# A Gelu gate streamed through one core: every transfer in one order on one queue

## The chip, the cores and the metric

The kernel runs on one core of a Trainium2 chip. The metric is the device time of one execution in microseconds (us), as the median of several runs. Of the core's engines the kernel uses ScalarE (ACT) for Gelu, VectorE (DVE) for the product, and two engines that issue transfers: SyncE (SP) and ScalarE. Each of these two has a queue of its own (q1 for SyncE and q10 for ScalarE in the profile); the packets of both are carried by the core's 16 DMA engines.

## What is computed

The input is x of shape (32, 512, 2048) in float32. The last axis is cut in two halves, and the output of shape (32, 512, 1024) is the Gelu of the first half times the second:

```
x1, x2 = x[..., :1024], x[..., 1024:]
out = 0.5 * x1 * (1 + erf(x1 / sqrt(2))) * x2
```

134.2 MB are read and 67.1 MB are written, each byte once.

## The kernel before, in words

The 16,384 rows of x are cut into 16 tiles of 1024 rows. Each of the 128 partitions takes R = 8 neighbouring rows of a tile (lines 26 to 29). So one tile puts 64 KB of input into each partition, contiguous in memory, and takes 32 KB of output from it. There are two input buffers, `x_bufs`, and two output buffers, `o_bufs` (lines 30 and 31); tile i uses number i % 2 of both.

A tile goes through four steps. `load` (line 48) brings it in from SyncE's queue. ScalarE computes Gelu of the first half of each row from the input buffer into the output buffer (line 87). VectorE multiplies the output buffer in place by the second half of each row (line 95). `store` (line 53) waits for the multiply and sends the output buffer out. Gelu and multiply work in steps of 5 and 3 rows (line 79), so that VectorE starts while ScalarE does the second step.

The order of the work is written by hand with semaphores, and every engine takes its instructions in program order:

- SyncE's queue has load 0 as two halves of four rows each and load 1 at once, and then load i + 2 as soon as both multiplies of tile i are done (line 114), which frees the input buffer. It also has the stores of the last two tiles (lines 104 and 110).
- ScalarE's queue has the stores of tiles 0 to 13 (lines 107 and 112). Since ScalarE waits for the multiply before it issues a store, its next Gelu comes after that.
- ScalarE begins tile i when `ready[i % 2]` has counted all transfers before it on that buffer pair: load i, which fills the input buffer, and store i - 2, which frees the output buffer (line 85).
- Tile 0 starts on the first half of its load. The first and the last tile work in steps of 2, 2 and 4 rows and are stored in two halves (lines 79 and 103 to 107).
- The first instruction on ScalarE's queue is a small transfer of 8 packets of 512 bytes from x into a tile that nobody reads (`opening`, line 63).

At the end SyncE waits for the stores counted by `tail_stored` (line 125).

Of the kernel before, what the change touches and what calls it, by code (L numbers as in the profile page):

```python
# [1 line left out]

# [4 lines left out]

GELU = mybir.ActivationFunctionType.Gelu


@with_exitstack
def kernel(
    ctx: ExitStack,
    tc: tile.TileContext,
    x: bass.AP,
    out: bass.AP,
):
    nc = tc.nc
    P = nc.NUM_PARTITIONS

    x_flat = x.flatten_outer_dims()
    out_flat = out.flatten_outer_dims()
    n_rows, dim = x_flat.shape
    half = dim // 2

    R = 8
    x_t = x_flat.rearrange("(n p r) d -> n p r d", p=P, r=R)
    o_t = out_flat.rearrange("(n p r) d -> n p r d", p=P, r=R)
    n_tiles = x_t.shape[0]
    x_bufs = [nc.alloc_sbuf_tensor(f"x{k}_tile", [P, R, dim], x.dtype) for k in range(2)]  # L30
    o_bufs = [nc.alloc_sbuf_tensor(f"o{k}_tile", [P, R, half], out.dtype) for k in range(2)]

    first = [nc.alloc_semaphore(f"first{j}") for j in range(2)]
    ready = [nc.alloc_semaphore(f"ready{k}") for k in range(2)]
    gelu_done = nc.alloc_semaphore("gelu_done")
    mul_done = nc.alloc_semaphore("mul_done")
    tail_stored = nc.alloc_semaphore("tail_stored")
    opened = nc.alloc_semaphore("opened")  # L40
    scrap = nc.alloc_sbuf_tensor("scrap_tile", [8, 128], x.dtype)
    n = {sem.name: 0 for sem in [*first, *ready, gelu_done, mul_done, tail_stored, opened]}

    def counted(ins, sem, by):
        ins.then_inc(sem, by)
        n[sem.name] += by

    def load(i, rows, sem):
        ins = nc.sync.dma_start(out=x_bufs[i % 2][:, rows, :], in_=x_t[i][:, rows, :])  # L49
        counted(ins, sem, 16)  # L50
        return ins

    def store(queue, i, rows, sem):
        queue.wait_ge(mul_done, n[mul_done.name])
        counted(
            queue.dma_start(out=o_t[i][:, rows, :], in_=o_bufs[i % 2][:, rows, :]), sem, 16
        )

    opening = nc.scalar.dma_start(out=scrap[:, :], in_=x_t[0][:8, 0, :128])
    counted(opening, opened, 16)
    for ins in (
        opening,
        load(0, slice(0, 4), first[0]),
        load(0, slice(4, 8), first[1]),
        load(1, slice(0, 8), ready[1]),
    ):  # L70
        tc.no_tile_sem_insts.add(ins.ins.name)
    tc.close()
    tc.compile()  # L73

    for i in range(n_tiles):
        k = i % 2
        last = i == n_tiles - 1
        pieces = i == 0 or last
        steps = ((0, 2), (2, 4), (4, 8)) if pieces else ((0, 5), (5, 8))
        for lo, hi in steps:  # L80
            rows = slice(lo, hi)
            if i == 0 and lo % 4 == 0:
                nc.scalar.wait_ge(first[lo // 4], 16)
            elif lo == 0:
                nc.scalar.wait_ge(ready[k], n[ready[k].name])
            counted(
                nc.scalar.activation(  # L87
                    out=o_bufs[k][:, rows, :], in_=x_bufs[k][:, rows, :half], func=GELU
                ),
                gelu_done,  # L90
                1,
            )
            nc.vector.wait_ge(gelu_done, n[gelu_done.name])
            counted(
                nc.vector.tensor_mul(  # L95
                    out=o_bufs[k][:, rows, :],
                    in0=o_bufs[k][:, rows, :],
                    in1=x_bufs[k][:, rows, half:],
                ),
                mul_done,  # L100
                1,
            )
            if pieces and hi % 4 == 0:
                if last:
                    store(nc.sync, i, slice(hi - 4, hi), tail_stored)
                else:
                    store(nc.scalar, i, slice(hi - 4, hi), ready[k])
        if not pieces:
            if i == n_tiles - 2:
                store(nc.sync, i, slice(0, R), tail_stored)  # L110
            else:
                store(nc.scalar, i, slice(0, R), ready[k])
        if i + 2 < n_tiles:
            nc.sync.wait_ge(mul_done, n[mul_done.name])
            load(i + 2, slice(0, R), ready[k])


    nc.scalar.wait_ge(opened, 16)
    nc.scalar.drain()  # L119
    for sem in (*first, *ready, opened):  # L120
        nc.scalar.sem_clear(sem)
    nc.vector.drain()
    nc.vector.sem_clear(gelu_done)
    nc.sync.sem_clear(mul_done)
    nc.sync.wait_ge(tail_stored, n[tail_stored.name]).then_inc(
        tail_stored, -n[tail_stored.name]
    )


# [1 line left out]
_INS = ['x']  # L131
_OUTS = [((32, 512, 1024), 'float32')]


# [23 lines left out]
```

## Time and profile before

| | before |
|---|---|
| median of 3 runs | 469.25 us (469.18 to 469.42) |
| span of the profiled execution | 467.8 us |
| own time of the profiled execution | not listed apart from the three runs |
| DVE busy | 140.5 us (30%), 34 multiplies |
| ACT busy | 115.5 us (25%), 34 Gelus and one table load |
| DMA traffic | 201.34 MB, mean 430 GB/s over the span |
| Gelu of 5 rows, of 3 rows | 4469 ns, 2747 ns |
| multiply of 5 rows, of 3 rows | 5493 ns, 3351 ns |
| time from issue to landing, median | 44.4 us for a load, 44.7 us for a store on ScalarE's queue |

The span is the time from the first to the last thing that the profile records of the execution; a run's time holds a little more around it. Busy shares are averages over the span. The share of a DMA queue is the time that its packets took, as a share of the span of all 16 DMA engines. The chain of waits is followed back from the last instruction, at each step to what released it. Idle time of ScalarE and VectorE costs nothing in itself as long as the transfers go on.

### The profile page before, as it was taken

What the parts mean: (1) busy time and instruction counts of PE and PEld (TensorE: products, weight loads), DVE (VectorE), ACT (ScalarE), POOL (GpSimd) and SP (SyncE); (2) the same over time, 40 slices, a digit from 0 to 9 for tenths busy, and PEclk for the clock granted to TensorE, in tenths of its full rate; (3) what the DMA queues carried; (4) which work ended last, traced back from release to release, by engine and by line L of the source; (5) the groups of instructions that cost most, each with busy time, mean ns of one, the idle gap of its engine ahead of it and who ended that gap; (6) DMA issues with size and microseconds to landing.
All of it is one profiled execution on the core that took longest, in us unless ns stands there. A gap on an engine that the chain in (4) does not pass through costs nothing.

```text
span 467.8 us, 154 instructions
## 1 busy us (share of the span) xinstructions
DVE 140.5 (30%) x34; ACT 115.5 (25%) x35; POOL 0.2 (0%) x4
## 2 busy tenths in 40 slices
DVE  0330515207051060511606115060150702507043
ACT  1320606041060410604105050050501506014060
POOL 0000000000000000000000000000000000000000
DMA  8999999999999999999999999999999999999988
GB/s 359 448 448 448 398 406 496 403 403 448 459 437 403 440 412 493 403 403 448 487 409 403 445 406 493 403 403 448 493 403 403 448 426 471 403 426 426 493 384 379
DMA packets 5057, 201.34 MB, mean 430 GB/s; under 512 B 568, under 2 KB 576, under 8 KB 576
## 3 DMA queue, kind: packets, MB, share of 16 engines
q1 hardware_dynamic: 2880, 142.61, 70.6%
q10 hardware_dynamic: 2176, 58.73, 29.1%
q14 instruction: 1, 0.01, 0.0%
HBM read 134.22 MB, written 67.11 MB: 430 GB/s over the span
## 4 chain that ended last, share of the span: by engine, by line
DMA 76%; DVE 14%; ACT 8%; ACTq 0%; SPq 0%; issue 0%
DMA out_dram<-o_tile 66%; DVE o_tile L95 14%; DMA x_tile<-in_x_dram 10%; ACT o_tile L87 8%; ACTq L119 0%; SPq L49 0%
## 5 line engine op out<-in xcount | busy, mean ns | idle before, releaser
L95 DVE TENSOR_TENSOR o_tile<-o_tile,x_tile 128x5120 f32<-128x5120 f32 (+3 forms) x34 | 140.5, 4171 | 319.7 <-ACT o_tile L87 319.7
L87 ACT ACTIVATE o_tile<-x_tile 128x5120 f32<-128x5120 f32 (+3 forms) x34 | 114.3, 3407 | 337.3 <-DMA out_dram<-o_tile 301.8
L87 ACT ACT_TABLE_LOAD x1 | 1.3, 1283 | 2.9 <-PEq L73 2.9
L142 POOL MEMSET const-bfloat16-1.0<- 128x1 bf16 x1 | 0.1, 102 | 0.0
L142 POOL MEMSET const-uint8-127<- 128x1 uint8 x1 | 0.1, 101 | 0.0
L142 POOL MEMSET const-float32-0.0<- 128x1 f32 x1 | 0.1, 99 | 0.2 <-issue 0.2
L142 POOL MEMSET const-float32-1.0<- 128x1 f32 x1 | 0.1, 98 | 0.0
## 6 DMA issues: line engine op xcount, KB each, us to landing
out_dram<-o_tile ACTq DMA_DIRECT2D x13, 4096.0 KB, 44.7
x_tile<-in_x_dram SPq DMA_DIRECT2D x2, 4096.0 KB, 16.7
out_dram<-o_tile ACTq DMA_DIRECT2D x2, 2048.0 KB, 34.4
out_dram<-o_tile SPq DMA_DIRECT2D x1, 4096.0 KB, 25.2
out_dram<-o_tile SPq DMA_DIRECT2D x2, 2048.0 KB, 7.8
x_tile<-in_x_dram SPq DMA_DIRECT2D x15, 44.4
scrap_tile<-in_x_dram ACTq DMA_DIRECT2D x1, 4.0 KB
```

The costliest lines, as they stand in the source:

```text
L87: nc.scalar.activation(out=o_bufs[k][:, rows, :], in_=x_bufs[k][:, rows, :half], func=GELU),
L95: nc.vector.tensor_mul(out=o_bufs[k][:, rows, :], in0=o_bufs[k][:, rows, :], in1=x_bufs[k][:, rows, half:],),
L142: nc = _bacc.Bacc("TRN2", target_bir_lowering=False, num_devices=1)
```

## The change

All transfers now go out on SyncE's queue, in one order: load 0, load 1, then store i and load i + 2 in turn, and at the end load 14, load 15, store 13, store 14 and store 15. Each tile has one load and one store: the halves of the first and the last tile are gone, and so are their steps of 2, 2 and 4 rows; every tile works in steps of 5 and 3 rows. The opening transfer and its tile are gone.

The output of the last tile, number 15, goes to the input buffer of tile 14 in place of its own output buffer, which tile 13's store still reads. It uses the first 32 KB of that buffer in each partition. ScalarE waits for tile 14's multiply before it begins there. Load 15 is issued ahead of store 13, and the last three stores are counted by `tail_stored`.

```diff
+    last = n_tiles - 1
+
+    def out_tile(i):
+        if i == last:
+            return x_bufs[(i - 1) % 2].rearrange("p r d -> p (r d)")[:, : R * half].rearrange(
+                "p (r d) -> p r d", r=R
+            )
+        return o_bufs[i % 2]
...
-    def store(queue, i, rows, sem):
-        queue.wait_ge(mul_done, n[mul_done.name])
-        counted(
-            queue.dma_start(out=o_t[i][:, rows, :], in_=o_bufs[i % 2][:, rows, :]), sem, 16
-        )
+    def store(i, rows, sem):
+        nc.sync.wait_ge(mul_done, n[mul_done.name])
+        counted(nc.sync.dma_start(out=o_t[i][:, rows, :], in_=out_tile(i)[:, rows, :]), sem, 16)
...
-    opening = nc.scalar.dma_start(out=scrap[:, :], in_=x_t[0][:8, 0, :128])
-    counted(opening, opened, 16)
-    for ins in (
-        opening,
-        load(0, slice(0, 4), first[0]),
-        load(0, slice(4, 8), first[1]),
-        load(1, slice(0, 8), ready[1]),
-    ):
+    for ins in (load(0, slice(0, R), ready[0]), load(1, slice(0, R), ready[1])):
...
-        last = i == n_tiles - 1
-        pieces = i == 0 or last
-        steps = ((0, 2), (2, 4), (4, 8)) if pieces else ((0, 5), (5, 8))
-        for lo, hi in steps:
+        nc.scalar.wait_ge(ready[k], n[ready[k].name])
+        if i == last:
+            nc.scalar.wait_ge(mul_done, n[mul_done.name])
+        for lo, hi in ((0, 5), (5, 8)):
...
-            if i == n_tiles - 2:
-                store(nc.sync, i, slice(0, R), tail_stored)
-            else:
-                store(nc.scalar, i, slice(0, R), ready[k])
-        if i + 2 < n_tiles:
+        if i == last - 2:
             nc.sync.wait_ge(mul_done, n[mul_done.name])
+            load(last, slice(0, R), ready[k])
+            store(i, slice(0, R), tail_stored)
+        elif i > last - 2:
+            store(i, slice(0, R), tail_stored)
+        else:
+            store(i, slice(0, R), ready[k])
             load(i + 2, slice(0, R), ready[k])
```

Gelu and multiply take their output from `out_tile(i)` in place of `o_bufs[k]`.

More of the change, by code (lines that the diff above doesn't have):

```diff
@@ L31 @@
     o_bufs = [nc.alloc_sbuf_tensor(f"o{k}_tile", [P, R, half], out.dtype) for k in range(2)]
-    first = [nc.alloc_semaphore(f"first{j}") for j in range(2)]
     ready = [nc.alloc_semaphore(f"ready{k}") for k in range(2)]
@@ L39 @@
     tail_stored = nc.alloc_semaphore("tail_stored")
-    opened = nc.alloc_semaphore("opened")
-    scrap = nc.alloc_sbuf_tensor("scrap_tile", [8, 128], x.dtype)
-    n = {sem.name: 0 for sem in [*first, *ready, gelu_done, mul_done, tail_stored, opened]}
+    n = {sem.name: 0 for sem in [*ready, gelu_done, mul_done, tail_stored]}
+    last = n_tiles - 1
[5 more added lines that the diff above has]
+        return o_bufs[i % 2]
     def counted(ins, sem, by):
@@ L76 @@
         k = i % 2
-        last = i == n_tiles - 1
-        pieces = i == 0 or last
-        steps = ((0, 2), (2, 4), (4, 8)) if pieces else ((0, 5), (5, 8))
-        for lo, hi in steps:
+        nc.scalar.wait_ge(ready[k], n[ready[k].name])
+        if i == last:
+            nc.scalar.wait_ge(mul_done, n[mul_done.name])
+        for lo, hi in ((0, 5), (5, 8)):
             rows = slice(lo, hi)
[L82 to L85, printed above, removed]
             counted(
                 nc.scalar.activation(
-                    out=o_bufs[k][:, rows, :], in_=x_bufs[k][:, rows, :half], func=GELU
+                    out=out_tile(i)[:, rows, :], in_=x_bufs[k][:, rows, :half], func=GELU
                 ),
@@ L95 @@
                 nc.vector.tensor_mul(
-                    out=o_bufs[k][:, rows, :],
-                    in0=o_bufs[k][:, rows, :],
+                    out=out_tile(i)[:, rows, :],
+                    in0=out_tile(i)[:, rows, :],
                     in1=x_bufs[k][:, rows, half:],
@@ L102 @@
             )
-            if pieces and hi % 4 == 0:
-                if last:
-                    store(nc.sync, i, slice(hi - 4, hi), tail_stored)
-                else:
-                    store(nc.scalar, i, slice(hi - 4, hi), ready[k])
-        if not pieces:
-            if i == n_tiles - 2:
-                store(nc.sync, i, slice(0, R), tail_stored)
-            else:
-                store(nc.scalar, i, slice(0, R), ready[k])
-        if i + 2 < n_tiles:
-            nc.sync.wait_ge(mul_done, n[mul_done.name])
+        if i == last - 2:
+            nc.sync.wait_ge(mul_done, n[mul_done.name])
+            load(last, slice(0, R), ready[k])
[4 more added lines that the diff above has]
+            store(i, slice(0, R), ready[k])
             load(i + 2, slice(0, R), ready[k])
-    nc.scalar.wait_ge(opened, 16)
     nc.scalar.drain()
-    for sem in (*first, *ready, opened):
+    for sem in ready:
         nc.scalar.sem_clear(sem)
```

## The prediction

> **What bounds the kernel now.** I read the busy rows and the queue table of the page first, then the chain of waits, then windows of exactly one tile, and last the records of single DMA packets (the trace holds for each one its queue, size, start and duration; a few of them are given below as numbers).
>
> The page, DMA row and queue table:
>
> ```profile
> DMA  8999999999999999999999999999999999999988
> ...
> DMA packets 5057, 201.34 MB, mean 430 GB/s; under 512 B 568, under 2 KB 576, under 8 KB 576
> ...
> q1 hardware_dynamic: 2880, 142.61, 70.6%
> q10 hardware_dynamic: 2176, 58.73, 29.1%
> ```
>
> q1 is SyncE's queue, q10 ScalarE's. Their shares add up to 99.7% of the time of all 16 DMA engines: these never rest, from the first load to the last store. The two shares also stand as the bytes do (142.61 / 70.6 = 2.02 and 58.73 / 29.1 = 2.02 MB per point), so a byte costs the same on either queue and in either direction.
>
> The chain of waits, two rounds of it:
>
> ```profile
> 113.70 44.67 DMA out_dram<-o_tile
> 158.37 0.02 issue
> 158.40 4.48 ACT o_tile L87
> 162.87 0.02 issue
> 162.90 8.77 DVE o_tile L95 x2
> 171.67 0.02 issue
> 171.69 44.69 DMA out_dram<-o_tile
> ```
>
> The chain runs through 4.48 us of Gelu and 8.77 us of multiply per round, 13.3 us with the steps between, and the page puts 22% of the span on these two. That is no time to be won: under it the DMA engines are busy with the other tile. Windows of one tile period show it:
>
> ```profile
> 120.00:149.00 29.00, 8.76 (x2) 7.12 (x2) 0.00 (x0) 1.00 1.00 434
> 149.00:178.00 29.00, 8.76 (x2) 7.12 (x2) 0.00 (x0) 1.00 1.00 434
> 178.00:207.00 29.00, 8.76 (x2) 7.12 (x2) 0.00 (x0) 1.00 1.00 434
> ```
>
> Columns: stretch, length, DVE busy, ACT busy, POOL busy, PE clock, DMA share, GB/s. Each 29.00 us moves one load and one store, 12.58 MB, at 434 GB/s with a DMA share of 1.00. So the kernel is 16 x 29.00 = 464.0 us of transfer plus a start. Only three things can move it: the pace of a packet, holes between packets, and the start.
>
> **The pace, in packets.** Each of the 16 engines moves 280 packets. From the start of one to the start of the next on the same engine it takes 2414 ns for 64 KB (a load), 1209 ns for 32 KB, 607 ns for 16 KB. A tile on one engine is 8 loads and 8 stores: 8 x (2414 + 1209) = 28.98 us; the two ends of transfers in it make the rest of 29.00. In the steady stretch 64 KB and 32 KB packets alternate, one from each queue.
>
> **The sum for the changed kernel**, against this execution: span 467.84 us, and 469.25 - 467.84 = 1.41 us around it (the median of three runs, which lie within 0.24; the profiled run's own time is not listed).
>
> - Load 0 in 64 KB packets in place of two halves of 32 KB: per engine 8 x (2 x 1209.4 - 2414) = 0.04 us less. Stores 0 and 15 in 32 KB in place of 16 KB: 16 x (2 x 607.1 - 1209.4) = 0.08 us less. Three transfer ends fewer per engine (17 loads and 18 stores become 16 and 16) at 6 ns (the packet that follows such an end on SyncE's queue starts after 1215 ns, not 1209): 0.02 us less. Together -0.13 us.
> - The order. SyncE's queue now holds load 0, load 1, store 0, load 2, store 1, load 3 and so on to load 14, load 15, store 13, store 14, store 15. The bytes are the same. A load has the engines alone for 8 x 2.414 = 19.3 us and a store for 8 x 1.209 = 9.7 us, in place of both together for 29.0. Cost nothing, as long as the queue never runs dry, which three covers decide:
>  - Start: tile 0 now waits for the whole of load 0 (before: for its first half). Data flow from about 3.0 us (first packets start at 2.2 to 2.75 and take 1.81 us on average, 0.60 more than 1.21), so load 0 has landed near 22.5, its second multiply ends 13.3 later at 35.8, and with 1.5 us from issue to first packet (issue at 0.73, packet at 2.21) store 0 could move at 37.3. Load 1 keeps the engines until 3.0 + 2 x 19.3 = 41.6: cover 4.3 us.
>  - Steady: store i-1 and load i+1 are issued 13.3 us after load i-1 landed, load i lands 29.0 after it: cover 15.7 - 1.5 = 14.2 us. Behind each SyncE wait stand store i and then load i+2, which needs the buffer that the same multiply frees; the load now comes one issue (0.34 us) later, inside the cover.
>  - Tail: load 15 no longer has work of its own behind it, but stores 13 and 14 do: 2 x 9.7 = 19.4 us against 13.3 + 1.5 for tile 15: cover 4.6 us. This cover exists because tile 15 writes into the other input buffer (free since tile 14's multiply) and so need not wait for store 13. Without it, 14.8 us would lie open.
> - DVE and ACT: 34 instructions of each become 32; their 140.5 and 115.5 us lie under the transfers. Tile 15's three steps with early stores become two and one store; covered by the 4.6 us above, and ScalarE's added wait for tile 14's multiply was met 29.0 - 13.3 us earlier. ScalarE loses 15 stores and the opening transfer (0.36 and 0.59 us of issue each); it idles two thirds of the time, so nothing. SyncE issues 32 transfers at 0.33 to 0.43 us each, under 14 us in 468.
> - The opening transfer (8 packets of 512 B, 25 ns each) starts at the same moment as load 0 and not ahead of it, so it can't have warmed anything for it. Unseen is load 0 without it: the first packets of most engines start within 0.25 us of each other, and half of that either way is my bound; I take nothing.
> - Slow packets early on. The 64 KB packets at 22.3 us average 2661 ns, those at 34.7 us 2476, those at 62.0 us 2437; after 68 us practically none is slow. Over both early tiles this adds 0.41 us per engine. They follow ScalarE's store issues at 19.3, 30.6 and 60.3 us by a few us, and the changed kernel issues stores early too, so I keep most: -0.1 (ends: -0.41 and 0).
>
> Sum: 469.25 - 0.13 - 0.1 = **469.0 us**, a change of -0.05%. The unknowns pull it to 469.25 - 0.13 - 0.41 - 0.27 = 468.4 at the low end (0.27: the last engine ends at 467.84, the mean of all at 467.57, as one engine has a hole of 0.30 us at 461.0) and to 469.4 at the high end.
>
> **What the trace doesn't show** is 64 KB packets behind one another: before, a store packet stands behind each. The nearest rows are 32 KB loads alone on the queue (4 to 22 us: 1209 ns, no drift) and stores alone (448.5 to the end: 1209 and 607 ns). By them 64 KB takes 2414 to 2 x 1209 = 2418; I take 2414. The far row is the mean of both early tiles, 2440.
>
> **Rivals.**
> 1. Loads alone run at the pace of the early tiles. There four fifths of the bytes are loads, in the steady stretch two thirds. Price: 128 packets x (2440 - 2414) = 3.3 us, 472.3. For it: the slow packets sit in the stretch with most load bytes. Against: from 40.8 to 59 us the mixture is the same and the pace is 2414; 32 KB loads alone don't slow. It would decide from (470.19 - 469.0) / 128 = 9 ns per packet on. Chance 0.12.
> 2. Slower by a hole at each change of direction. On one queue a store's first packet stands right behind a load's last one, with the semaphore write between; before, the other queue had a packet ready. There are 27 such changes. Priced by the one latency that the trace shows openly, the 0.60 us of the first packets: 27 x 0.60 = 16.2 us, 485.2. It decides from (470.19 - 469.0) / 27 = 44 ns per change. Against: when ScalarE's queue was empty (load 0's halves and load 1, up to 22 us; store 14 and the two halves of store 15) SyncE's queue passed four ends of transfers at 6 ns each, and between the two queues the direction turns at every packet without cost. Not shown: end and turn on one queue together. Chance 0.07. The Trainium skill speaks for this rival: "DMA: Bandwidth & Descriptors", Anatomy of one DMA, puts a fixed cost of about 2.0 us on each DMA, most of it the confirmation of the last write. Laid end to end for 32 transfers that would be an estimate of 64 us; the 6 ns of the trace say that the engines take up the next transfer meanwhile, at least within one direction.
> 3. Faster: the slow packets and the hole at 461 go entirely, and load 0 starts 0.1 us earlier: 468.3. All have to come together. Chance 0.08.
> 4. It doesn't do what it says. The listing of instructions by engine has all 32 transfers on SyncE in the order above and none on ScalarE; what could fail is that the queue takes so many at once. At most three transfers are outstanding, as were load 0's halves and load 1 before. Chance 0.01, in with rival 2.
>
> **How the numbers follow.** The forecast (468.4 to 469.4) has 0.72. One measurement of this kernel can tell about 0.2% from no change, 0.94 us; the forecast lies inside. Faster 0.08, within 0.2% 0.72, slower 0.20 (rivals 1, 2 and 4). The range goes from 468.3, below which rival 3 ends, to 472.5, just over rival 1; what is left out is rival 2.
>
> **What would show it.** One queue with 99% of the engines' time; Gelu starts 29.0 us apart in the middle; 64 KB packets at 2414 ns inside a load; each load's last and store's first packet 1215 to 1225 or 2420 ns apart. Slow 64 KB packets throughout would show rival 1, holes every 9.7 and 19.3 us rival 2. A DMA share under 1 between 35 and 42 us, or in the last 10, would show that a cover was too short, and the sum wrong there.

## The result and the profile after

The changed kernel takes 474.06 us (median of 5 runs, 473.52 to 474.74) against 469.31 us beside it: a ratio of 1.0100, with a 95% interval of 1.0085 to 1.0115. It is slower by 1.0%, where no change to be seen was forecast. The profiled run took 474.74 us with a span of 473.4 us (before: 467.8).

The page after, DMA rows and queue:

```profile
DMA  8999999999999999999999999999999999999996
GB/s 354 443 443 385 424 432 443 443 415 465 396 462 443 390 435 429 446 443 404 471 399 471 443 385 435 424 451 437 426 449 399 471 407 418 443 443 432 418 429 266
...
q1 hardware_dynamic: 4608, 201.33, 98.9%
```

One queue, as intended, and DMA engines that are busy 98.9% of the time in place of 99.7%. By this row the transfers still bound the kernel and nothing stands still. Two things give the loss away. The bytes are the same and the busy share is almost the same in a longer span, so packets must have become longer. And the last slice is at 266 GB/s (before: 379).

The start of each Gelu after, from the timeline (start, length, engine, line, form, idle before and what ended it):

```profile
43.30 7.12 ACT L75 ACTIVATE o_tile<-x_tile 128x5120 f32<-128x5120 f32 x2 [13.48 <-DMA x_tile<-in_x_dram]
72.62 7.12 ACT L75 ACTIVATE o_tile<-x_tile 128x5120 f32<-128x5120 f32 x2 [22.20 <-DMA x_tile<-in_x_dram]
102.19 7.12 ACT L75 ACTIVATE o_tile<-x_tile 128x5120 f32<-128x5120 f32 x2 [22.44 <-DMA x_tile<-in_x_dram]
132.12 7.12 ACT L75 ACTIVATE o_tile<-x_tile 128x5120 f32<-128x5120 f32 x2 [22.81 <-DMA x_tile<-in_x_dram]
...
425.06 7.12 ACT L75 ACTIVATE o_tile<-x_tile 128x5120 f32<-128x5120 f32 x2 [21.92 <-DMA x_tile<-in_x_dram]
```

Tiles 1 to 14 start on average (425.06 - 43.30) / 13 = 29.37 us apart, and unevenly (29.32, 29.57, 29.93), where before they came every 29.00 us. Each of these Gelus waited for its load, which has landed only when all 16 DMA engines have brought their part, so this is the pace of the slowest engine.

The end, in windows of 5 us (stretch, length, DVE, ACT and POOL busy, PE clock, DMA share, GB/s; a short window counts some packets of its neighbours, so a share is good to some 0.1):

```profile
458.40:463.40 5.00, 0.00 (x0) 0.00 (x0) 0.00 (x0) 1.00 0.99 426
463.40:468.40 5.00, 0.00 (x0) 0.00 (x0) 0.00 (x0) 1.00 1.00 433
468.40:473.40 5.00, 0.00 (x0) 0.00 (x0) 0.00 (x0) 1.00 0.18 79
```

In the last 5 us most DMA engines have nothing left to do. The packet records say which (packet times in this document are set so that the last packet ends with the span; on the profile's own time axis they lie about 0.4 us earlier): ten of the 16 end between 468.65 and 468.74 us, and six at 470.51, 471.29, 471.33, 472.25, 472.38 and 473.41 us. Before, all 16 ended within 0.44 us.

One engine's packets around the first store, from the same records (start in us, KB, duration in ns):

```
kernel before      24.83 store 16  611 | 25.44 load 64 2451 | 27.89 store 16  611
changed kernel     36.55 load  64 2439 | 38.98 load 64 3727 | 42.71 store 32 1213 | 43.92 store 32 1213
later, for 64 KB   2418 as a rule, but up to 3300 where a load's last packet stands before a store
```

Nothing is lost within a load (64 KB packets behind one another: 2414 ns apart), within a store (1209 ns), or from a store to the next load (6 ns). What is longer is the last packet of a load before a store. Summing each packet's duration over its usual one (2418, 1213, 611 ns), and the time in which an engine has no packet, gives a ledger per engine (mean of 16, in us):

| | before | after | difference |
|---|---|---|---|
| packets at their usual duration | 464.98 | 464.77 | -0.21 |
| no packet before the first one | 2.37 | 2.38 | 0.01 |
| first packets longer | 0.59 | 0.59 | 0.00 |
| packets longer, 15 to 50 us (the first store) | 0.37 | 1.19 | 0.82 |
| packets longer, after 50 us | 0.07 | 1.51 | 1.44 |
| no packet, from the first one to 20 us before the end | 0.12 | 0.07 | -0.05 |
| no packet, last 20 us | 0.30 | 3.72 | 3.42 |
| span | 467.84 | 473.41 | 5.57 |

The rows add up to 0.8 to 1.0 us more than the span, since records of neighbouring packets overlap by 3 to 4 ns. The 3.42 us at the end are what the other engines, the ten early ones above all, wait for the slowest. So three terms: a dearer first store, later stalls, and the spread of the engines that these cause, as they fall on some engines only. Lost time (longer packets, the first one included, and ends of transfers) adds up to 7.3 us on the engine that ends last and to 2.2 to 2.8 us on the ten early ones. Each engine carries 8 of the 128 packets of every transfer, and none takes over another's.

### The profile page after: what moved, and what is told of

Its sections match the earlier page's. It is cut to its first block, busy times and chain, and to the rows that moved or that the text cites. A ratio compares the mean times of both kernels' runs of the same rounds, so it can differ in the third digit from the quotient of the medians.

```text
span 473.4 us, 144 instructions
## 1 busy us (share of the span) xinstructions
DVE 140.2 (30%) x32; ACT 115.2 (24%) x33; POOL 0.2 (0%) x4
## 3 DMA queue, kind: packets, MB, share of 16 engines
q1 hardware_dynamic: 4608, 201.33, 98.9%
## 4 chain that ended last, share of the span: by engine, by line
DMA 73%; DVE 14%; ACT 8%; DVEq 1%; SPq 1%; issue 0%
DMA x_tile<-in_x_dram 73%; DVE o_tile L83 13%; ACT o_tile L75 7%; DVE x_tile L83 1%; ACT x_tile L75 1%; DVEq L104 1%; SPq L60 0%; SPq L54 0%
## 5 line engine op out<-in xcount | busy, mean ns | idle before, releaser
L83 DVE TENSOR_TENSOR o_tile<-o_tile,x_tile 128x5120 f32<-128x5120 f32 (+1 forms) x30 | 131.4, 4421 | 306.9 <-ACT o_tile L75 306.9
L75 ACT ACTIVATE o_tile<-x_tile 128x5120 f32<-128x5120 f32 (+1 forms) x30 | 106.8, 3608 | 321.7 <-DMA x_tile<-in_x_dram 321.7
L83 DVE TENSOR_TENSOR x_tile<-x_tile 128x5120 f32<-128x5120 f32 (+1 forms) x2 | 8.8, 4422 | 10.6 <-ACT x_tile L75 10.6
L75 ACT ACTIVATE x_tile<-x_tile 128x5120 f32<-128x5120 f32 (+1 forms) x2 | 7.1, 3608 | 12.2 <-DMA x_tile<-in_x_dram 12.2
```

Of the source, the lines that this page charges most:

```text
L75: nc.scalar.activation(out=out_tile(i)[:, rows, :], in_=x_bufs[k][:, rows, :half], func=GELU),
L83: nc.vector.tensor_mul(out=out_tile(i)[:, rows, :], in0=out_tile(i)[:, rows, :], in1=x_bufs[k][:, rows, half:],),
```

## The experiments

The question was what makes the last packet of a load long. A *turn* below is a place where loads end and stores begin. Each run is compared with the kernel before, run beside it (469.2 to 469.3 us every time). Four theories came up one after the other. **A**: a queue that holds loads and stores is late at each turn, and a second queue fills the hole. **A'**: such a queue is late at each turn, whatever else is there. **H**: a store is late after a stretch without stores. **P**: it is late where all engines load for a long phase and then all store at full rate, be it on one queue or two. Further letters are rivals, which the expectations explain. In all runs "stalls" are the ledger's longer packets, as a mean per engine, and the "price of the first store" is the ledger's row from 15 to 50 us. Every run that puts stores and the next load on different queues also gives the load's queue its own wait for the multiply. "..." in a cut of code stands for lines left out.

### Undoing one part: stores on ScalarE's queue

```diff
-        nc.sync.wait_ge(mul_done, n[mul_done.name])
...
+        queue = nc.scalar if i < last - 1 else nc.sync
+        queue.wait_ge(mul_done, n[mul_done.name])
...
+            nc.sync.wait_ge(mul_done, n[mul_done.name])
             load(i + 2, slice(0, R), ready[k])
```

> The changed kernel with one part undone: stores 0 to 13 are issued by ScalarE on its own queue again; whole first and last tile, no opening transfer, last output in the other input buffer all stay. Theory A (on one queue a store that stands right behind a load begins late; a second queue's packets fill that): 468.5 to 469.2 us, all 16 engines done within 1 us of each other, 64 KB packets 2414 ns apart. Theory B (the removed halves and opening transfer cost the time at both ends): about 474 us.

Measured: 474.86 us, ratio 1.0119 (1.0104 to 1.0134). The time alone would fit theory B. The profile says otherwise: stalls after 50 us are 0.08 us in place of 1.51, and the time is lost in one hole near the end, 5.4 us without a packet on average:

```profile
453.60:458.60 5.00, 4.88 (x1) 2.75 (x2) 0.00 (x0) 1.00 0.76 328
458.60:463.60 5.00, 3.88 (x2) 0.00 (x0) 0.00 (x0) 1.00 0.24 105
463.60:468.60 5.00, 0.00 (x0) 0.00 (x0) 0.00 (x0) 1.00 0.98 419
```

DVE is at work on tile 15 and the DMA engines wait for it. With store 13 on the other queue, it shares the engines with load 15 and lands with it; then only store 14 (9.7 us) covers the 14.8 us of tile 15. That is a fault of this experiment, which a later run mends.

### Both directions on both queues

```diff
-        ins = nc.sync.dma_start(out=x_bufs...
+        ins = (nc.sync if i % 2 == 0 else nc.scalar).dma_start(out=x_bufs...
...
+        queue = nc.scalar if i % 2 and i < last else nc.sync
...
```

> Even tiles have load and store on SyncE's queue, odd tiles on ScalarE's (store 15 on SyncE's). Each queue changes from load to store and back as in the changed kernel, but the other queue has packets waiting meanwhile. Theory A: the late store begins are filled by the other queue: 468.5 to 470 us. Rival C (any queue that carries both directions loses the time, filled or not): 472 to 475 us, with slow last packets of loads before a store.

Measured: 488.19 us, 1.0404 (1.0389 to 1.042), beyond either theory, for a reason that neither had:

```profile
42.00:57.00 15.00, 10.52 (x3) 14.11 (x4) 0.00 (x0) 1.00 0.08 35
```

Loads 0 and 1 are on two queues, share the engines packet by packet and land together at 42 us, so nothing is left to move while tile 0 is computed: 15 us of it. That is 14.9 us of the 19.0; another 2.0 us are long packets between 60 and 70 us, soon after the transfers set out again. The rest bears on the theories. After 70 us, 1.7 us of stalls remain although there is always a second queue, so theory A's "filled by a second queue" fell. They say more: store 3 is issued on ScalarE's queue at 131.34 us, and the long load packets, at 133.5 us, are on SyncE's; store 4 is issued on SyncE's queue at 165.27 us, and they are on ScalarE's, at 167.5 us. So here the stall isn't on the queue that turns, which speaks against theory A' as well.

### More turns, and a control

```diff
-            store(i, slice(0, R), ready[k])
-            load(i + 2, slice(0, R), ready[k])
+            for lo in (0, 4):
+                store(i, slice(lo, lo + 4), ready[k])
+                load(i + 2, slice(lo, lo + 4), ready[k])
```

> One queue as in the changed kernel, but store i and load i+2 of tiles 0 to 12 go out as half store, half load, half store, half load: about 26 changes from load to store where the changed kernel has 14, same bytes. Smaller packets and 52 more semaphore updates alone add an estimated 1.0 + 1.0 x 13/16 us at 4.8 ns per split packet, some 1.5 us. Theory A with a price per change: the slow engines lose some 5 us more than the changed kernel, 479 to 482 us. Rival D (the loss goes with the bytes or with time, not with the changes): 475 to 476 us, as the run with grouped halves.

The control issues both halves of the store, then both of the load.

> Control of the run before: the same halves, in the order half store, half store, half load, half load, so that the number of changes is that of the changed kernel. Theories A and D both: 475 to 476 us, the changed kernel plus 1.5 us for smaller packets.

Measured: 474.18 us (1.0108, 1.0093 to 1.0123) with twice the turns, 475.00 us (1.012, 1.0103 to 1.0137) for the control. Twice the turns cost nothing: 0.95 us of stalls over 26 turns after the first, 37 ns each, against 0.85 us over 13 for the control and 1.51 us over 13 in the changed kernel (116 ns). A fixed price per turn fell here. Phases half as long didn't lower the sum of the stalls either, and in the run with twice the turns they aren't spread evenly: all but 0.02 us of the 0.95 come before 290 us, though the turns go on in the same way. The spread at the end is there in both (2.5 and 3.7 us without a packet).

### The tail mended

```diff
...
+        queue = nc.scalar if i < last - 2 else nc.sync
...
```

> Stores 0 to 12 on ScalarE's queue, store 13 again behind load 15 on SyncE's queue with stores 14 and 15, as in the changed kernel. In the run with all stores but two on ScalarE's queue the DMA engines stood still for 5.1 us near the end, since load 15 and store 13 landed together and only store 14 covered tile 15's work. Theory A' (a queue that turns from load to store loses time and pulls the engines apart; the tail of that run was its own fault): that 5.1 us goes and 469.7 to 470.3 us remain, the time before less 0.2 for larger packets plus 0.8 for the dearer first store. Rival B' (the changed kernel loses its time in the shape of its two ends): 473 to 475 us.

Measured: 470.04 us, 1.0019 (1.0009 to 1.0028), as expected; theory B fell. Stalls after 50 us: 0.01 us. No packet in the last 20 us: 0.43. All engines end within 0.8 us. The Gelu starts are even again:

```profile
131.56 7.12 ACT L76 ACTIVATE o_tile<-x_tile 128x5120 f32<-128x5120 f32 x2 [21.94 <-DMA out_dram<-o_tile]
160.55 7.12 ACT L76 ACTIVATE o_tile<-x_tile 128x5120 f32<-128x5120 f32 x2 [21.87 <-DMA out_dram<-o_tile]
189.54 7.12 ACT L76 ACTIVATE o_tile<-x_tile 128x5120 f32<-128x5120 f32 x2 [21.87 <-DMA out_dram<-o_tile]
```

The period is 29.0 us. This run differs from the changed kernel only in the queue of 13 stores, and they are 4.0 us of the 4.75. The 0.7 us left to the kernel before are as much as the first store costs more, 1.15 us here against 0.37; a later run tests that.

The end of this run holds a second answer. No store packet starts from 414.1 to 438.7 us: the end of load 14 and all of load 15 have the 16 engines to themselves, and then store 13 follows on the same queue. That is a turn of theory A', and yet the longest load packet there takes 2426 ns, 8 ns over the usual, and the stalls from 425 to 446 us are 0.003 us.

### Is it the first write, or the size of packets?

An early small store from ScalarE's queue, with the tail in one order and with one queue:

```diff
...
+    nc.scalar.dma_start(out=o_t[last][:, 0, :128], in_=scrap[:, :]).then_inc(early, 16)
+    nc.scalar.wait_ge(early, 16)
```

> The run above with one store of 128 x 512 B from ScalarE's queue at about 2 us, into rows of the last tile that are written again at the end. It asks what the 1.2 us are by which every engine's last packet before the very first store is longer. Theory X (the first write to the output pays something once): the small store pays it under load 0, and the run is 0.7 to 1.1 us shorter than the one above, 468.8 to 469.4 us. Rival Y (the price is that of the first large store beside the loads, whatever went before): as the run above.

> The changed kernel, all large transfers on SyncE's queue, with the same early small store from ScalarE's queue. Theory X: the 1.2 us before the first store go, 473.0 to 473.5 us, the later stalls and the spread stay. Rival Y: 474 us, no change. If the later stalls go as well, the first common stall is what sets them off, and the time would be about 469 us.

Measured: 470.46 us (1.0027, 1.0015 to 1.0039) and 474.04 us (1.0102, 1.0085 to 1.0119). With the stores on their own queue the first store's price stays (1.03 us); with one queue it fell to 0.39 us, but later stalls (1.19) and the wait at the end (3.36) stayed, and the time with them. So having written before isn't what the time hangs on; why the price was lower in the one run stays open. The first of the two is a little longer than the run without the small store: its packets take turns with 64 KB ones, it landed only near 25 us, and Gelu 0 waited for it (25.09 in place of 22.55 us).

Loads in halves, so that packets on both sides of a turn have 32 KB:

```diff
             store(i, slice(0, R), ready[k])
-            load(i + 2, slice(0, R), ready[k])
+            for lo in (0, 4):
+                load(i + 2, slice(lo, lo + 4), ready[k])
```

> One queue as in the changed kernel, whole stores, but each of loads 2 to 14 as two halves in 32 KB packets, so that the packets on both sides of a change are of 32 KB. Rival S (what stalls is the step from 64 KB to 32 KB packets, not the turn from load to store): stalls after 50 us vanish, and the time is about 470.5 us. Theory A' (the turn): stalls and spread of the engines stay, 473 to 475 us, though a shorter packet may be stretched less.

Measured: 473.68 us, 1.009 (1.0075 to 1.0105); stalls 0.87 us (1.51 in the changed kernel), and 2.2 us without a packet at the end. Rival S fell: the stalls are fewer, but not gone.

### Which queue, and which use of it

The opening transfer put back:

> The run with its tail in one order (stores 0 to 12 on ScalarE's queue, 470.04 us) plus the opening transfer of the kernel before, 8 packets of 512 B read on ScalarE's queue at the start. Asks whether the dearer first store (1.15 us per engine, 0.37 before) comes from ScalarE's queue not having been used. If so: 469.2 us and a first price of about 0.4 us. If not: 470.0 us.

The queues swapped (loads from ScalarE, stores from SyncE, the tail in one order on ScalarE's queue):

> Loads on ScalarE's queue, stores 0 to 12 on SyncE's, stores 13 and 14 behind load 15 on ScalarE's queue, store 15 on SyncE's. Theory A' (mixing loads and stores on one queue is what costs, not which engine issues): no slow packets between 50 and 440 us, 469.8 to 470.4 us. Rival Q (stores on SyncE's queue are slow as such): 472 us or more, slow packets before stores as in the changed kernel.

Measured: 470.06 us (1.0011, 1.0000 to 1.0022) and 470.11 us (1.0012, 1.0001 to 1.0024), each with 0.01 to 0.02 us of stalls after 50 us and 1.17 to 1.18 us at the first store. The opening transfer is worth nothing here, and swapping the two queues changes nothing. Rival Q fell.

### Two queues, but a stretch of loads alone

```diff
-            load(i + 2, slice(0, R), ready[k])
...
+            for lo in (0, 2, 4, 6):
+                load(i + 2, slice(lo, lo + 2), ready[k])
```

with stores 0 to 12 on ScalarE's queue.

> The run with its tail in one order, with loads 2 to 14 in quarters of 16 KB packets. The two queues hand over packet by packet, so the 8 store packets of a tile are through after 8 x (1209 + 607) = 14.5 us and some 14.5 us of loads alone follow before the next store, as in the changed kernel, yet no queue holds both. Packets and updates add 1.5 us + 39 x 6 ns per engine, 1.7 us in all: 471.7 us if nothing stalls. Theory A' (the turn from load to store on one queue): no stalls after 50 us, 471.4 to 472.0 us. Rival H (any store that follows a stretch of loads alone is late, whatever queue it is on): 0.7 to 1.5 us of stalls per engine after 50 us, 473 us or more.

Measured: 476.51 us, 1.0148 (1.0117 to 1.0178). Stalls after 50 us: 3.20 us, 2.23 of them on load packets and 0.95 on store packets. In mid-run no queue turns here, and yet the stalls are there, so theory A' fell.

Store 0 in two halves:

```diff
-            store(i, slice(0, R), ready[k])
+            for lo, hi in ((0, 4), (4, 8)) if i == 0 else ((0, 8),):
+                store(i, slice(lo, hi), ready[k])
```

> The run with its tail in one order, store 0 alone as two halves in 16 KB packets, both issued at the same moment as before. If the price of the first store goes with its packets (0.37 us in the kernel before, with 16 KB): 469.2 to 469.5 us. If it goes with the moment or with the stretch of loads ahead of it: 470.0 us, price 1.1 us.

Measured: 474.69 us, 1.0116 (1.0078 to 1.0153). The first price fell only to 0.88 us, and the run is 4.7 us longer than the one without this edit. The timeline tells why:

```profile
56.57 0.36 ACTq L61 DMA_DIRECT2D out_dram<-o_tile  x1
88.62 7.12 ACT L76 ACTIVATE o_tile<-x_tile 128x5120 f32<-128x5120 f32 x2 [38.22 <-DMA out_dram<-o_tile]
...
101.91 0.36 ACTq L61 DMA_DIRECT2D out_dram<-o_tile  x1
102.32 7.12 ACT L76 ACTIVATE o_tile<-x_tile 128x5120 f32<-128x5120 f32 x2 [6.58 <-DVE o_tile L84]
```

Store 0 now has 16 packets per engine against 8 of a load. The queues hand over packet by packet, so it takes two loads' time and holds up its buffer and Gelu 2 to 88.62 us. Load 3 is through 2 us later, store 1 alone is left, and the engines run dry: 3.05 us without a packet, and 1.27 us of stalls when stores and loads set out again near 101 us.

### A trickle of small stores

One queue for all large transfers, and per tile 16 pieces of 64 B per engine from ScalarE's queue, one between every two large packets; the control has small loads in their place; a third run has the trickle before the first store only, with the tail in one order.

```diff
...
+    nc.scalar.dma_start(out=o_t[last][:, 0:2, :16], in_=scrap[:, :, :]).then_inc(small, 16)
...
+        if 1 <= i <= last - 2:
+            nc.scalar.wait_ge(small, 16 * i)
+            nc.scalar.dma_start(out=o_t[last][:, 0:2, :16], in_=scrap[:, :, :]).then_inc(small, 16)
```

> The changed kernel, all large transfers in one order on SyncE's queue, plus a trickle on ScalarE's queue: per tile one store of 256 pieces of 64 B into rows of the last tile that are written again later, 16 per engine; the two queues hand over packet by packet, so one goes between every two large packets and there is no stretch of loads without a store. Price of the trickle at 10 to 25 ns each: 14 x 16 = 224 pieces, 2.2 to 5.6 us. Theory H (a store is late after a stretch of loads alone, on whatever queue): stalls after 50 us fall from 1.5 to under 0.3 us per engine, the price of the first store falls well under 0.5, the engines end within 1 us of each other; time 470.5 to 474 us by the price of the trickle. Theory A' (one queue that holds both): stalls and spread stay, 476 us or more.

> Control of the run above: the same trickle with small loads of x in place of small stores. Theory H: stalls (1.5 us), price of the first store (1.2 us) and spread (over 3 us) stay as in the changed kernel, 476 to 479 us. Rival T (any second queue at work cures it, by breaking up the stretch of large packets): as the run above.

> The run with its tail in one order (470.04 us) plus a single trickle of that kind at the start, 16 pieces of 64 B per engine, which lasts until store 0 begins. Theory H: the price of the first store falls from 1.15 to under 0.4 us, 469.0 to 469.4 us, level with the kernel before. If the price stays: 470.1 to 470.4 us.

Measured: 478.37 us (1.0204, 1.0187 to 1.0221), 476.17 us (1.015, 1.0135 to 1.0165) and 469.93 us (1.0015, 1.0005 to 1.0024). The pieces take 11 ns each, 2.5 us per engine in all. Stalls after 50 us are 3.5 and 4.0 us, and the first store's price is 0.88, 0.97 and 0.94 us. A trickle of stores keeps no store from being late, so theory H in this form fell too. The first two runs are no clean test of it: Gelu of the next tile waits there until the pieces have landed, 30 us after their issue, and this wait ended 292 and 282 us of ScalarE's idle time, so the trickle also moved the tiles' work. The third run has it at the start only, and there the first store's price stays at 0.94 us. That stalls grew in the course of these two runs (most of them come after 370 us with small stores, after 220 us with small loads) isn't explained.

### Short phases on one queue, matched packets on two

```diff
-            store(i, slice(0, R), ready[k])
-            load(i + 2, slice(0, R), ready[k])
+            for r in range(R):
+                store(i, slice(r, r + 1), ready[k])
+                load(i + 2, slice(r, r + 1), ready[k])
```

> One queue as in the changed kernel, but store i and load i+2 of tiles 0 to 12 go out row by row in turn: 8 packets of 4 KB out (about 1.2 us per engine), 8 of 8 KB in (2.4 us), and so on, so that the direction turns as often as on the kernel before's two queues, though on one queue. Small packets and 182 more updates alone cost an estimated 4.7 ns x 1456 + 182 x 6 ns = 7.9 us per engine. Theory P (what costs is a long phase in which all engines load, followed by one in which all store): stalls after 50 us under 0.3 us per engine and the engines end within 1.5 us of each other; 477 to 478 us. Theory A' (a turn on one queue costs, each time): eight times the changed kernel's turns, 1.5 us of stalls or more, 480 us or more.

Measured: 479.55 us, 1.0218 (1.0204 to 1.0232). The time missed the range: packets at their usual duration come to 476.5 us, 11.8 more than in the changed kernel where 7.9 were estimated. But stalls after 50 us are 0.12 us in place of 1.51, with eight times as many turns on the same single queue. Of the engines, 15 end within 0.6 us of each other and one 1.9 us after them, which misses the expected 1.5 us and sets the time; why that one lags isn't known.

The control of the quarter loads, with the stores in quarters too:

> Control of the run with quarter loads (476.51 us, 3.2 us of stalls): the stores of tiles 0 to 12 in quarters too, 32 packets of 8 KB beside 32 of 16 KB, so that the two queues again finish a tile together and no stretch of loads alone is left. Smaller store packets add some 13 x 24 x 4.7 ns + 39 x 6 ns = 1.7 us. Theory P: stalls after 50 us fall to under 0.3 us, 473 to 474 us. If the stalls of the quarter loads came from the many small transfers: 3 us or more of stalls, 478 us.

Measured: 473.10 us, 1.008 (1.0064 to 1.0095), with 0.02 us of stalls after 50 us where unmatched quarters had 3.20, and a perfectly even pace (29.26 us, from the smaller packets):

```profile
130.94 7.12 ACT L76 ACTIVATE o_tile<-x_tile 128x5120 f32<-128x5120 f32 x2 [22.14 <-DMA out_dram<-o_tile]
160.20 7.12 ACT L76 ACTIVATE o_tile<-x_tile 128x5120 f32<-128x5120 f32 x2 [22.14 <-DMA out_dram<-o_tile]
189.46 7.12 ACT L76 ACTIVATE o_tile<-x_tile 128x5120 f32<-128x5120 f32 x2 [22.14 <-DMA out_dram<-o_tile]
```

Both runs hold to theory P as far as stalls go: one queue without stalls (short phases), two queues with stalls (quarter loads, with long stretches of loads alone), and two without (packet by packet). But two things keep it from being shown as the cause.

- **A long phase isn't enough.** The turn from load 15 to store 13, after 20 to 25 us without a store, cost 0.003 us or less in all of six runs: the one with its tail in one order, and those that add to it the early small store, the opening transfer, the swapped queues, the one trickle, or the first tile in pieces (below). In the changed kernel itself the turn from load 13 to store 12 cost nothing. So a stall falls at such a turn, but not every such turn stalls; what else it takes stays open.
- **Phase and packet shrink together.** Row by row, the packets are of 8 and 4 KB. No run has short phases of large packets, so the two weren't told apart. The quarter loads, with 16 KB packets, stall, so smaller load packets alone are no cure.

### The first tile in pieces

Tail in one order, and tile 0 as before: load in halves, steps of 2, 2 and 4 rows, store in halves, the first at 19 us.

```diff
...
+            if i == 0 and hi % 4 == 0:
+                store(i, slice(hi - 4, hi), ready[k])
...
```

> The run with its tail in one order (470.04 us) with tile 0 as in the kernel before: its load in two halves, steps of 2, 2 and 4 rows, its store in two halves, the first of them at 19 us in place of 36. Kernel before, then, with a whole last tile that uses the other input buffer and without the opening transfer. If the head alone is what the dearer first store hangs on, its price falls from 1.15 to 0.4 us: 469.1 to 469.4 us, level with the kernel before. If not, 470.0 us.

Measured: 469.37 us, 1.0002 (0.9993 to 1.0011), level with the kernel before; first price 0.48 us. The 0.7 us of the first store hang on the shape of the first tile. Whether on its coming 17 us earlier or on its smaller pieces isn't settled; pieces alone at the later time lowered the price only from 1.15 to 0.88 us. Here the whole last tile in the other buffer is as good as three steps and two halves. No version beat the kernel before.

## Why the prediction was wrong, step by step

- **What bounds the kernel**: right. Every microsecond lost is a longer packet or a packet that a DMA engine doesn't have.
- **Larger packets, fewer ends**: -0.13 us forecast, -0.21 us in the ledger.
- **"The order ... Cost nothing, as long as the queue never runs dry"**: this step failed. The queue practically never ran dry (0.07 us without a packet in mid-run), and the order cost 1.4 us of stalls all the same. The step took the pace of packets for a property of the packet. In the kernel before loads and stores alternate at every packet; the change makes phases of 19.3 and 9.7 us, and the trace before shows a long phase of loads followed by a store in one place only, the first store. Its slow packets were read as a consequence of store issues and priced at 0.3 us; they were the one row that spoke of the phases, and 0.37 us there became 1.19. That the coarse order costs this time is shown by undoing it (470.04 us, stalls 0.01 us); why some of its turns cost up to 0.9 us on an engine and others nothing stays open.
- **The sum ran over the mean engine.** To stalls of 2.7 us per engine come 3.4 us of waiting at the end, because the stalls are uneven and the slowest engine ends the kernel. No term of the sum stood for spread; before, it was 0.44 us at the end, and there was nothing to set it off.
- **Covers**: the one at the start held. The one at the tail, 4.6 us, was eaten by 5.3 us of spread when load 15 landed: the early engines waited 0.1 to 0.5 us for store 15, issued at 457.69 us. The 1.5 us from issue to first packet, a term of these covers, are 1.0 us on the profile's own time axis (packet at 1.74 us, where 2.21 was read); that changes no verdict here.
- **Rival 1** (64 KB packets slow by themselves) was wrong: 2414 ns behind one another.
- **Rival 2** (a hole at each change of direction) had the place, with a chance of 0.07, and the wrong price and cause: from loads to stores it costs 0.1 us in the mean after the first time and from stores to loads 6 ns, where 0.60 us had been assumed for both; and the one queue by itself is not the cause (0.12 us of stalls row by row). The evidence brought against it, four ends of transfers at 6 ns, was of one direction, as the prediction said itself, and the turn at every packet was of short phases.
- **The fixed cost** of about 2.0 us per DMA, which the Trainium skill gives in "DMA: Bandwidth & Descriptors", Anatomy of one DMA, is a fit to transfers issued from GpSimd, which this kernel has none of. No such time is lost by the engines here: from a store to the next load they lose 6 ns.

The range (468.3 to 472.5) missed by 1.6 us: its upper end stood on rival 1 and left rival 2 out.

## What to carry to other kernels

Where transfers bound a kernel, ask not only for bytes, packets and a queue that's never empty, but how the directions are mixed in time. Loads on one queue and stores on another, with as many packets per tile on each, kept 16 engines in step for 400 us; all transfers on one queue in an order with no gap cost 0.9% (474.06 against 470.04 us), and unmatched packet counts on two queues cost more (476.51 us). Price the slowest DMA engine rather than the mean one, and where the present kernel does once what the new one will do always, let that row set the range, though not as a fixed price: here it was 0.37 us once, and became 1.19 us once and 0 to 0.2 us at each later turn.

## What the runs showed of the hardware

- The two queues hand over packet by packet, whatever the packets' sizes: 64 KB against 32 or 16 KB, and 64 B pieces each waiting for a large packet. The Trainium skill says that a DMA engine goes round its queues packet by packet ("DMA: Bandwidth & Descriptors", Queues, rings and completion order), with typically 9 to 17 descriptors to a packet. The traces agree on the alternation; what alternates here is single records, one 64 B piece of 11 ns per large packet. So a transfer of many small packets beside one of few large ones is slow to land (16 KB in 30 us), which held up Gelu 0 with the early small store, Gelu 2 with store 0 in halves, and most Gelus with the trickle.
- The Trainium skill says on that page, under Issuing engines are not separate DMA queues, that issuing from several engines at once only saves issue time. Here the measurement differs: 13 stores moved from one queue to the other made 474.06 into 470.04 us. By the runs it's not the queue as such that does it, but the mixture in time that two queues give for nothing when each has as many packets per tile.
- Which engines stall is uneven: in the changed kernel six of 16 fell behind, losing up to 0.9 us at one turn, and at one turn (load 13 to store 12) no engine stalled. What in the memory or the DMA engines makes the last packet of a load long isn't settled by these runs; nor why the stalls prefer engines that are late already (after 150 us the early engines' last load packets keep to their usual 2418 ns within 0.03 us, but for a few near 437 us).
